# Two row blocks of w_out loaded during the mix, and the first two token tiles multiplied block by block in four banks

## The chip, the core and the metric

The kernel runs on one core of one Trainium2 chip, in one launch. The metric is the device time of the whole program in microseconds. The kernel before takes 2972.97 us, the median of three runs (2965.73 to 2975.23).

## The reference, cut to what matters

The program computes two transformer-like blocks for 1024 tokens of width 1024, in float32. The change lies in the first block, between its two branches and its mixture of experts:

```python
mixed = (jax.nn.sigmoid(g_rwkv) * (o_rwkv @ w_branch_rwkv[l])
         + jax.nn.sigmoid(g_diff) * (o_diff @ w_branch_diff[l]))     # "the mix"
x = x + mixed @ w_out[l]                                             # "mix_out": 1024 x 1024 weights
x = x + hierarchical_moe(rms_norm(x, norm_ffn[l]), ...)              # router, then 32 experts, top 2
```

## The kernel before, in words

Each float32 operand of a large product is split into a rounded part, `hi`, and a rest, `lo` (`split`, lines 188 to 191: ScalarE writes `hi`, then VectorE writes `lo`). A product is then three TensorE matmuls, hi by hi (line 276), the one operand's hi by the other's lo (277), and lo by hi (278).

**The mix** (`mix`, line 812) goes over eight feature blocks `f` and two branches `b`. For each pair it loads 128 columns of a branch weight, splits them, and makes two half products of 12 matmuls each (token halves of 512) into two PSUM buffers with the tag `mm`. VectorE takes each out of PSUM and multiplies it by the gate (837, 839). The result is split straight into `mT[j]`, one tile of 8 KB a partition for each of the eight token tiles `j` (842, 843).

**mix_out** (line 852) loads the eight row blocks `k` of `w_out` (128 x 1024 each, 512 KB), one by one, into two raw buffers `wr`, and splits each into a hi and a lo tile `mx_w`. Then, for each token tile `j`, it forms two products of 512 columns, each of 8 x 3 matmuls, adds them to a tile `xr` of `x` (872), and hands it to the callback: store as `x1`, RMS norm, store as `mo_hn`, transpose, router logits, top 2 (`tile_in`, from line 934). This is the routing of a tile; it is interleaved on all engines with the products of the next tiles.

**The ring.** `mT` are eight of the ten buffers of a pool called the ring (`ring_tile`, line 885). Later users take the buffers in turn: the weights of the experts, loaded by `half` (line 1032) in pieces of 1 MB. Before the change the next two buffers, the ninth and tenth, hold the two halves of the first expert's `w_gate`.

**What sets the order.** The program is recorded in the order of the code. A scheduler with a timeline model then fixes the order of the instructions on each engine; an engine executes its own list in order, and each DMA is issued by SyncE (SP) in the order of its list. A DMA that waits therefore holds back all that stand behind it. Memory of a closed pool is used again by the next one; an instruction that writes there waits for the last reader or writer of that stretch.

Of the kernel before, what the change touches and what calls it, by code (L numbers as in the profile page):

```python
# [11 lines left out]
F32 = mybir.dt.float32  # L12
F32R = mybir.dt.float32r
# [9 lines left out]
T = 1024  # L23
D = 1024
KT = 8
# [783 lines left out]
    es.close()  # L809


def mix(K, o_ds, gate_d, mT):

    nc, tc, ap = K.nc, K.tc, K.ap
    with K.pool(name="mx_i", bufs=1) as ip, K.pool(name="mx_g", bufs=1) as gp, K.pool(name="mx_o", bufs=1) as op:
        oT = [[p.tile([128, 4, T], F32R, name=f"mx_oT{b}{i}") for i in range(2)] for b, p in enumerate((ip, op))]

        def load(b):  # L820
            for k in range(4):
                raw = ip.tile([128, T], F32, name=K.name("mx_raw"), tag="raw", bufs=3)
                nc.sync.dma_start(raw, o_ds[b].rearrange("(k p) t -> k p t", p=128)[k])
                K.split(oT[b][0][:, k], oT[b][1][:, k], raw)

        gts = {}

        def branch(b, f):
            if b == 0:
                gts[f] = gp.tile([128, 2, T], F32, name=K.name("gt"), tag="gt", bufs=3)  # L830
            gt = gts[f]
            w = K.load_w(ip, ap[("w_branch_rwkv", "w_branch_diff")[b]][0], [(f * 128, 128)], kt=4, raw_bufs=3, bufs=4)
            nc.sync.dma_start(gt[:, b], gate_d[b * 1024 + f * 128:b * 1024 + (f + 1) * 128, :])
            for hf in range(2):
                hs = slice(hf * 512, (hf + 1) * 512)
                p = K.gemm_fm(w, 0, 128, oT[b], hf * 512, kt=4)
                nc.vector.scalar_tensor_tensor(gt[:, b, hs], gt[:, b, hs], 1.0, p, op0=OP.add, op1=OP.mult)
                if b:
                    nc.vector.tensor_add(gt[:, 0, hs], gt[:, 0, hs], gt[:, 1, hs])
                    for j in range(hf * 4, hf * 4 + 4):  # L840
                        g, m = gt[:, 0, j * 128:(j + 1) * 128], mT[j]
                        nc.scalar.activation(m[:, 0, f], g, AF.Copy, scale=0.5)
                        nc.vector.scalar_tensor_tensor(m[:, 1, f], g, 0.5, m[:, 0, f].bitcast(F32), op0=OP.mult, op1=OP.subtract)

        load(0)
        branch(0, 0)
        load(1)
        for f in range(8):
            if f < 7:
                branch(0, f + 1)  # L850
            branch(1, f)


def mix_out(K, mT, x, cb):

    nc, tc, ap = K.nc, K.tc, K.ap
    with K.pool(name="mx_w", bufs=1, side="right") as wp:
        his, los = [], []
        for k in range(KT):
            raw = wp.tile([128, D], F32, name=K.name("wr"), tag="wr", bufs=2)  # L860
            nc.sync.dma_start(raw, ap["w_out"][0, k * 128:(k + 1) * 128, :])
            hi, lo = [wp.tile([128, 1, D], F32R, name=f"mx_w{i}{k}") for i in range(2)]
            K.split(hi[:, 0], lo[:, 0], raw)
            his.append(hi)
            los.append(lo)
        w = Parts(his, los, 1)
        for j in range(8):
            xr = wp.tile([128, D], F32, name=K.name("xr"), tag="xr", bufs=3)
            nc.sync.dma_start(xr, x[j * 128:(j + 1) * 128, :])
            for c in range(2):  # L870
                p = K.gemm_tm(w, (mT[j][:, 0], mT[j][:, 1]), 0, 512, c0=c * 512)
                nc.vector.tensor_add(xr[:, c * 512:(c + 1) * 512], xr[:, c * 512:(c + 1) * 512], p)
            cb(j, xr)


# [9 lines left out]
def ring_tile(K, ring, *shape, dt=F32):  # L885

    return ring.tile([128, *shape], dt, name=K.name("we"), tag="w", bufs=RING)
# [1018 lines left out]
def s5_scratch(K, dp):  # L1906
    d = {
        "keep": dp.tile([128, S5Keep.N], F32, name="s5d_keep"),
        "ca": dp.tile([128, 4, 2, 4, 144], F32, name="s5d_ca"),
        "km": dp.tile([32 * 16 * 240], F32, name="s5d_km"),  # L1910
        "wt": dp.tile([128, 4, 2, 4, 128], F32, name="s5d_wt"),
        "ro": dp.tile([128, 4, 2, 4, 128], F32, name="s5d_ro"),
    }
    with K.pool(name="s5z", bufs=1) as zp:
        zero = zp.tile([128, 960], F32, name="s5_zero")
        K.nc.vector.memset(zero, 0.0)
        K.nc.sync.dma_start(dap(d["km"], 0, [[960, 128], [1, 960]]), zero)
    return d
# [261 lines left out]
def branches(K, x, xs_d, gate_d, or_d, od_d):  # L2180

    tc = K.tc
    with K.pool(name="hT", bufs=1) as hp, K.pool(name="bd", bufs=1, space=DRAM) as dd:
        tab_d, qk_d, pd = (dd.tile(list(s), F32, name=f"d_{n}") for n, s in
                            (("tab", (2, 8, 128, 128)), ("qk", (T, 1024)), ("pd", (T, 1536))))
        hT = [hp.tile([128, KT, T], F32R, name=f"hT{i}") for i in range(2)]
        with K.pool(name="wp", bufs=1) as wp, K.pool(name="rp", bufs=1) as rp:
            first_w = lambda i, p: K.load_w_steps(wp, K.ap["w_in"][0], [(RWKV_ORDER[i] * 128, 128)], part=KT, raw_pool=p, raw_bufs=2)
            after, ws = norm_in(K, x, "norm_mix", hT, first_w)
            rwkv_proj(K, hT, wp, xs_d, rp, ws)  # L2190
            with K.issue_after(*after):
                rope_tables(K, tab_d)
                zeros = rwkv_scratch(K, dd)
            rwkv_core(K, xs_d, or_d, zeros)
            rope = norm_rope(K, rp, pd, tab_d, qk_d)
            proj_diff(K, hT, wp, rp, pd, lambda c: rope if c > 1 else iter(()))
            gates = proj_gate(K, hT, wp, rp, gate_d)
            for _ in range(5):
                next(gates)
            diff_attn(K, qk_d, pd[:, 1024:1536], od_d, gates)  # L2200
            for _ in gates:
                pass
# [53 lines left out]
def program(tc, nc, cst, out, **ap):  # L2256
    K = Kern(tc, ap, cst)
    K.setup()
    dd = K.es.enter_context(K.pool(name="dd", bufs=1, space=DRAM))
    dt = lambda n, *s: dd.tile(list(s), F32, name=f"d_{n}")  # L2260
    xs_d, gate_d = dt("xs", 1792, T), dt("gate", 2048, T)
    or_d, od_d, x1_d, y_d, x3_d = dt("or", 512, T), dt("od", 512, T), dt("x1", T, D), dt("y", 2 * T, D), dt("x3", T, D)
    mixT_d, part_d = dt("mixT", 1536, T), dt("part", T, D)
    branches(K, ap["x"][0], xs_d, gate_d, or_d, od_d)
    d5 = s5_scratch(K, dd)
    rings = ExitStack()
    ring = rings.enter_context(K.pool(name="mo_w", bufs=1, side="right"))
    mT = [ring_tile(K, ring, 2, KT, 128, dt=F32R) for _ in range(8)]
    mix(K, [or_d, od_d], gate_d, mT)

    def x1_tiles(cb):
        def put(j, x1):
            nc.sync.dma_start(x1_d[j * 128:(j + 1) * 128, :], x1)
            cb(j, x1)
        mix_out(K, mT, ap["x"][0], put)

    pps = ExitStack()
    pp = Ple(K, pps, ring, dt("pp", T // 2, D))

    def beside():  # L2280
        yield from s5_prep(K, d5)
        yield from pp.late()

    moe(K, ring, x1_tiles, y_d, pp.early(), beside(), pp.weights)
    es = ExitStack()
    hp = es.enter_context(K.pool(name="hU", bufs=1))
    hT = [hp.tile([128, KT, T], F32R, name=f"hU{i}") for i in range(2)]
    ple(K, pp, x1_d, y_d, x3_d, hT)
    pps.close()
    rings.close()  # L2290
    mixers(K, es, hT, d5, mixT_d, part_d, x3_d, out)
    K.close()
# [14 lines left out]
```

## Time and profile before

| what | us |
|---|---|
| median of three runs | 2972.97 |
| their range | 2965.73 to 2975.23 |
| the profiled execution | 2955.07 |
| its span, first to last instruction | 2953.3 |
| TensorE busy in it | 2786.6 (94%) |
| mean granted TensorE clock | 0.970 of full speed |

The profile is of one execution, 17.9 us shorter than the median of the runs. Times in its rows count from the start of the span. PE is TensorE's matmul, PEld its weight load, DVE is VectorE, ACT ScalarE, SP SyncE's DMA queue. In the stage of interest, the mix ends at about 1042 us, mix_out lasts to about 1168 us, and the experts follow.

### The profile page before, as it was taken

What the parts mean: (1) busy time and instruction counts of PE and PEld (TensorE: products, weight loads), DVE (VectorE), ACT (ScalarE), POOL (GpSimd) and SP (SyncE); (2) the same over time, 40 slices, a digit from 0 to 9 for tenths busy, and PEclk for the clock granted to TensorE, in tenths of its full rate; (3) what the DMA queues carried; (4) which work ended last, traced back from release to release, by engine and by line L of the source; (5) the groups of instructions that cost most, each with busy time, mean ns of one, the idle gap of its engine ahead of it and who ended that gap; (6) DMA issues with size and microseconds to landing.
All of it is one profiled execution on the core that took longest, in us unless ns stands there. A gap on an engine that the chain in (4) does not pass through costs nothing. (4 is left out here: it accounts for less than half of the span.)

```text
span 2953.3 us, 47258 instructions
## 1 busy us (share of the span) xinstructions
PE 2786.6 (94%) x18410; PEld 2290.6 (78%) x18410; DVE 1962.3 (66%) x3826; ACT 1314.0 (44%) x2167; POOL 229.2 (8%) x193
## 2 busy tenths in 40 slices
PE   6999999988998989979999999999999999999998
PEld 5888888765776868668777776678888899987776
DVE  4436787654455655769988888569745666768653
ACT  4223332223454221658877877334432335543431
POOL 0000111000000000112122110000000000000000
PEclk9999999987998999989999999999999999999999
DMA  5333343323213465879999996542234444357333
GB/s 182 103 96 90 108 129 115 106 64 99 65 61 139 159 196 186 281 261 376 378 339 336 351 361 241 185 126 88 88 111 129 132 133 146 99 164 225 109 125 132
DMA packets 378146, 503.31 MB, mean 170 GB/s; under 512 B 86039, under 2 KB 234422, under 8 KB 377918
## 3 DMA queue, kind: packets, MB, share of 16 engines
q1 hardware_dynamic: 347742, 458.63, 47.1%
q0 software_dynamic: 11296, 24.57, 2.3%
q10 hardware_dynamic: 18880, 17.05, 1.7%
q8 instruction: 146, 2.39, 0.3%
q14 instruction: 82, 0.67, 0.1%
HBM read 410.26 MB, written 106.68 MB: 175 GB/s over the span
## 5 line engine op out<-in xcount | busy, mean ns | idle before, releaser
L191 DVE TENSOR_TENSOR wh<-we,wh 128x1024 fp32r<-128x1024 f32 x384 | 451.2, 1219 | 62.5 <-ACT wh L190 60.9
L190 ACT ACTIVATE wh<-we 128x1024 fp32r<-128x1024 f32 x384 | 385.7, 1057 | 47.3 <-PE b L278 29.7
L276 PE MATMUL mm<-wh,hU 128*128 128x256 f32 (+1 forms) x768 | 221.7, 291 | 6.8 <-DVE z L1385 4.0
L277 PE MATMUL mm<-wl,hU 128*128 128x256 f32 (+1 forms) x768 | 220.3, 287 | 2.5 <-DVE wl L191 2.5
L278 PE MATMUL mm<-wh,hU 128*128 128x256 f32 (+1 forms) x768 | 218.6, 285 | 0.0
L278 PE MATMUL mm<-wh,hT 128*128 128x256 f32 (+1 forms) x640 | 211.6, 331 | 0.0
L276 PE MATMUL mm<-wh,hT 128*128 128x256 f32 (+1 forms) x640 | 203.0, 334 | 2.3 <-ACT ye L1082 2.3
L276 PE MATMUL mm<-hT,wh 128*128 128x512 f32 x480 | 194.4, 406 | 4.1 <-DVE xs L321 3.9
L277 PE MATMUL mm<-hT,wh 128*128 128x512 f32 x480 | 190.9, 398 | 0.0
L278 PE MATMUL mm<-hT,wl 128*128 128x512 f32 x480 | 189.1, 394 | 0.0
L190 ACT ACTIVATE wh<-wr 128x1024 fp32r<-128x1024 f32 (+2 forms) x102 | 100.9, 992 | 196.9 <-PE mm L277 152.9
L191 DVE TENSOR_TENSOR wl<-wr,wh 128x1024 fp32r<-128x1024 f32 (+2 forms) x102 | 115.9, 1137 | 91.5 <-ACT wh L190 84.4
L276 PEld LDWEIGHTS mm<-wh,hU 128*128 128x128 f32 x768 | 146.0, 191 | 11.0 <-DVE z L1385 5.0
L277 PEld LDWEIGHTS mm<-wl,hU 128*128 128x128 f32 x768 | 146.8, 191 | 5.7 <-DVE wl L191 3.3
L278 PEld LDWEIGHTS mm<-wh,hU 128*128 128x128 f32 x768 | 146.8, 191 | 1.4 <-issue 1.4
L276 PEld LDWEIGHTS mm<-wh,hT 128*128 128x128 f32 x640 | 121.0, 190 | 17.4 <-issue 3.4
L278 PEld LDWEIGHTS mm<-wh,hT 128*128 128x128 f32 x640 | 121.6, 190 | 16.1 <-issue 4.9
L276 PE MATMUL mm<-hU,wh 128*128 128x512 f32 x320 | 129.0, 403 | 4.5 <-ACT wh L190 4.5
L277 PE MATMUL mm<-hU,wh 128*128 128x512 f32 x320 | 127.5, 398 | 0.0
L278 PE MATMUL mm<-hU,wl 128*128 128x512 f32 x320 | 126.6, 396 | 0.0
L276 PEld LDWEIGHTS mm<-hT,wh 128*128 128x128 f32 x480 | 91.3, 191 | 30.2 <-DVE xs L321 4.4
L277 PE MATMUL mm<-wl,hT 128*128 128x256 f32 x384 | 111.1, 290 | 0.0
(704 smaller groups left out, 7062.7 us busy)
## 6 DMA issues: line engine op xcount, KB each, us to landing
we<-w_gate SPq DMA_DIRECT2D x64, 1024.0 KB
we<-w_up SPq DMA_DIRECT2D x64, 1024.0 KB
we<-w_down SPq DMA_DIRECT2D x64, 1024.0 KB
wr<-w_in SPq DMA_DIRECT2D x86, 512.0 KB
d_gate<-gz SPq DMA_DIRECT2D x32, 256.0 KB
gt<-d_gate SPq DMA_DIRECT2D x16, 512.0 KB
x<-d_x SPq DMA_DIRECT2D x16, 512.0 KB
dec<-sd_cum SPq DMA_DIRECT2D x16, 512.0 KB
```

The lines of the kernel that those rows point to most:

```text
L190: self.nc.scalar.activation(hi, src, AF.Copy)
L191: self.nc.vector.tensor_sub(lo, src, hi.bitcast(F32))
L276: nc.tensor.matmul(out, a[0], b[0], start=first, stop=False)
L277: nc.tensor.matmul(out, a[0], b[1], start=False, stop=False)
L278: self.last = nc.tensor.matmul(out, a[1], b[0], start=False, stop=last)
```

## The change

Two of the eight row blocks of `w_out` are loaded and split during the mix: a call `ahead`, after `f == 3` in the code, takes two of the mix's own raw buffers and writes hi and lo into the last two ring buffers. mix_out then loads only the row blocks 2 to 7, with four raw buffers instead of two. The first two token tiles are multiplied together: for each row block, both tiles and both column halves, in four PSUM banks (two with the tag `mm`, two with the tag `b`). Tiles 2 to 7 go as before.

```diff
-def mix(K, o_ds, gate_d, mT):
+def mix(K, o_ds, gate_d, mT, ahead):
...
+            if f == 3:
+                ahead(rawt)
+
+def w_out_rows(K, k, raw, hi, lo):
+    K.nc.sync.dma_start(raw, K.ap["w_out"][0, k * 128:(k + 1) * 128, :])
+    K.split(hi[:, 0], lo[:, 0], raw)
...
-def mix_out(K, mT, x, cb):
+def mix_out(K, mT, x, w2, cb):
...
-        for k in range(KT):
-            raw = wp.tile([128, D], F32, name=K.name("wr"), tag="wr", bufs=2)
+        his, los = [[t[i] for t in w2] for i in range(2)]
+        for k in range(len(w2), KT):
+            raw = wp.tile([128, D], F32, name=K.name("wr"), tag="wr", bufs=4)
...
-        for j in range(8):
...
+        xrs = [load(j) for j in range(2)]
+        ps = [[K.ps(tag=t) for _ in range(2)] for t in ("mm", "b")]
+        for k in range(KT):
+            for j in range(2):
+                for c in range(2):
+                    K.mm3(ps[j][c], (mT[j][:, 0, k], mT[j][:, 1, k]), w.at(k, slice(c * 512, (c + 1) * 512)), k == 0, k == KT - 1)
+        for j in range(2):
             for c in range(2):
+                add(xrs[j], c, ps[j][c])
+            cb(j, xrs[j])
+        for j in range(2, 8):
...
+    wo = [ring_tile(K, ring, 2, 1, D, dt=F32R) for _ in range(2)]
+    wo = [(t[:, 0], t[:, 1]) for t in wo]
+    def ahead(raw):
+        for k in range(2):
+            w_out_rows(K, k, raw(), *wo[k])
```

The scheduler moves more than the code does. In the rows below, `we_9604` and `we_9605` are `mT[0]` and `mT[1]`, `we_9612` and `we_9613` the split row blocks 0 and 1 of `w_out`. On SP, in the middle of the mix, the order before is:

```order
L823 DMA mx_raw_9689<-d_od 128x1024 [waits DMAHW5_49,DVE_49]
L233 DMA wr_9996<-w_branch_diff 128x4x128 [waits DMAHW3_49,DVE_49]
L233 DMA wr_10050<-w_branch_rwkv 128x4x128 [waits DMAHW0_49,DVE_49]
L1032 DMA we_11656<-w_gate 128x4x512 [waits PE_49]
L1032 DMA we_11658<-w_gate 128x4x512 [waits DMAHW6_49,PE_49]
```

and of the change:

```order
L827 DMA mx_raw_9691<-d_od 128x1024 [waits DMAHW5_49,DVE_49]
L862 DMA mx_raw_10051<-w_out 128x1024 [waits DMAHW6_49,DMAHW3_49,DVE_49]
L862 DMA mx_raw_10055<-w_out 128x1024 [waits DMAHW7_49,DVE_49]
L233 DMA wr_9998<-w_branch_diff 128x4x128 [waits DVE_49]
L233 DMA wr_10060<-w_branch_rwkv 128x4x128 [waits DMAHW0_49,DVE_49]
```

The two loads of `w_out` now stand right behind the last input of the mix, and the two of `w_gate` are gone from here; they stand behind all loads of `w_out`. On DVE, the change puts the two lo parts behind the last split of the first feature block, ahead of the next two products that it takes out of PSUM:

```order
L847 SCALAR_TENSOR_TENSOR we_9611<-gt_9643,we_9611 128x128
L191 TENSOR_TENSOR we_9612<-mx_raw_10051,we_9612 128x1024
L191 TENSOR_TENSOR we_9613<-mx_raw_10055,we_9613 128x1024
L841 SCALAR_TENSOR_TENSOR gt_9784<-gt_9784,mm_9806 128x512
L191 TENSOR_TENSOR wl_9964<-wr_9963,wh_9966 128x512
L841 SCALAR_TENSOR_TENSOR gt_9695<-gt_9695,mm_9827 128x512
```

The row L841 of `mm_9806` is the old row L837 that followed at once. On PE, six matmuls of token tile 1 by row block 0 go in behind the product `mm_9827`, and six by row block 1 some 24 matmuls later:

```order
L278 MATMUL mm_9827<-mx_oT_9625,wl_9821 128x512
L276 MATMUL b_10483<-we_9612,we_9605 128x512
L276 MATMUL b_10484<-we_9612,we_9605 128x512
L277 MATMUL b_10483<-we_9612,we_9605 128x512
L278 MATMUL b_10483<-we_9612,we_9605 128x512
L277 MATMUL b_10484<-we_9612,we_9605 128x512
L278 MATMUL b_10484<-we_9612,we_9605 128x512
L276 MATMUL mm_9850<-mx_oT_9625,wh_9823 128x512
```

So 12 matmuls of mix_out now lie inside the mix. On SP, where the mix ends, the order before is:

```order
L861 DMA wr_10431<-w_out 128x1024 [waits DMAHW3_49,DVE_49]
L861 DMA wr_10437<-w_out 128x1024 [waits DMAHW4_49]
L869 DMA xr_10479<-x 128x1024 [waits DMAHW5_49,PE_49]
L869 DMA xr_10623<-x 128x1024 [waits DMAHW6_49]
L869 DMA xr_10767<-x 128x1024 [waits DMAHW7_49]
L861 DMA wr_10443<-w_out 128x1024 [waits DMAHW3_49,DMAHW0_49,DVE_49]
```

and of the change:

```order
L862 DMA wr_10441<-w_out 128x1024 [waits DMAHW3_49,DVE_49,PE_49]
L862 DMA wr_10447<-w_out 128x1024 [waits DMAHW4_49,DVE_49]
L862 DMA wr_10453<-w_out 128x1024 [waits DMAHW5_49]
L862 DMA wr_10459<-w_out 128x1024 [waits DMAHW6_49]
L882 DMA xr_10477<-x 128x1024 [waits DMAHW7_49]
L882 DMA xr_10479<-x 128x1024 [waits DMAHW0_49]
L882 DMA xr_10765<-x 128x1024 [waits DMAHW1_49]
L862 DMA wr_10465<-w_out 128x1024 [waits DMAHW3_49,DMAHW2_49,DVE_49]
```

The wait for PE has moved from the first load of `x` to the first load of `w_out`: the pool is laid out anew, and its first raw buffer now lies where the mix keeps its last lo weights. By its count this wait, like the old one of `xr_10479`, is for the last product of the mix. On PE, behind the mix, the change has:

```order
L278 MATMUL mm_10482<-we_9612,we_9604 128x512
L276 MATMUL mm_10482<-we_9613,we_9604 128x512
L277 MATMUL mm_10482<-we_9613,we_9604 128x512
L278 MATMUL mm_10482<-we_9613,we_9604 128x512
L276 MATMUL mm_10481<-mx_w_10442,we_9604 128x512
L276 MATMUL mm_10482<-mx_w_10442,we_9604 128x512
L276 MATMUL b_10483<-mx_w_10442,we_9605 128x512
L276 MATMUL b_10484<-mx_w_10442,we_9605 128x512
L277 MATMUL mm_10481<-mx_w_10443,we_9604 128x512
L278 MATMUL mm_10481<-mx_w_10442,we_9604 128x512
```

The first four of these rows end the 12 matmuls of token tile 0 by row blocks 0 and 1; with `mx_w_10442` (hi of row block 2) begin the 72 of both tiles by row blocks 2 to 7, 12 for each, four of them before the lo part is needed.

## Rows read from the trace of the kernel before

**Rows 1.** The page: busy us and share of the span, by engine.
```profile
PE 2786.6 (94%) x18410; PEld 2290.6 (78%) x18410; DVE 1962.3 (66%) x3826; ACT 1314.0 (44%) x2167; POOL 229.2 (8%) x193
```

**Rows 2.** Windows: us from:to, length, busy us (instructions) by engine, clock, DMA share, GB/s.
```profile
969.00:1042.00 73.00, 72.24 (x317) 59.16 (x316) 47.76 (x114) 20.01 (x70) 1.92 (x3) 1.00 0.47 146
1042.00:1070.00 28.00, 17.74 (x49) 10.44 (x50) 13.42 (x23) 9.15 (x12) 0.00 (x0) 0.88 0.55 195
1070.00:1168.00 98.00, 98.00 (x530) 83.91 (x529) 50.92 (x237) 18.66 (x46) 3.88 (x7) 1.00 0.55 177
```

**Rows 3.** Timeline of PE: start us, us, engine, line, operation [idle before].
```profile
1034.73 0.39 PE L278 MATMUL mm<-mx_oT,wl 128*128 128x512 f32 x1
...
1041.53 0.39 PE L278 MATMUL mm<-mx_oT,wl 128*128 128x512 f32 x1
1045.31 0.73 PE L276 MATMUL mm<-mx_w,we 128*128 128x512 f32 x2 [3.39 <-ACT mx_w L190]
...
1069.72 0.50 PE L276 MATMUL mm<-mx_w,we 128*128 128x512 f32 x1 [0.32 <-DVE xr L872]
```

**Rows 4.** Waits in 1042 to 1070 us: us in total, times, longest.
```profile
ACT mx_w L190 <- DMA wr<-w_out: 14.2, 5, 5.0
```

**Rows 5.** Timeline of SP: DMAs issued at the end of the mix.
```profile
1038.76 0.85 SPq L861 DMA_DIRECT2D wr<-w_out  x2
1041.72 1.28 SPq L869 DMA_DIRECT2D xr<-x  x3
...
1054.74 0.33 SPq L861 DMA_DIRECT2D wr<-w_out  x1
...
1062.37 0.33 SPq L861 DMA_DIRECT2D wr<-w_out  x1
```

**Rows 6.** Timeline of ACT and PE: the sixth and the eighth row block.
```profile
1060.03 1.06 ACT L190 ACTIVATE mx_w<-wr 128x1024 fp32r<-128x1024 f32 x1 [1.75 <-DMA wr<-w_out]
...
1065.84 1.06 ACT L190 ACTIVATE mx_w<-wr 128x1024 fp32r<-128x1024 f32 x1 [1.69 <-DMA wr<-w_out]
...
1066.95 0.73 PE L276 MATMUL mm<-mx_w,we 128*128 128x512 f32 x2 [0.29 <-ACT mx_w L190]
1068.21 0.50 PE L277 MATMUL mm<-mx_w,we 128*128 128x512 f32 x1 [0.53 <-DVE mx_w L191]
```

**Rows 7.** Windows inside mix_out's first tile, columns as in rows 2.
```profile
1042.00:1047.00 5.00, 1.17 (x4) 0.69 (x5) 4.42 (x15) 2.80 (x6) 0.00 (x0) 1.00 1.02 415
1047.00:1050.00 3.00, 3.00 (x9) 2.36 (x8) 0.65 (x1) 0.00 (x0) 0.00 (x0) 0.52 0.89 268
...
1054.00:1057.00 3.00, 3.00 (x9) 2.32 (x8) 0.71 (x1) 0.00 (x0) 0.00 (x0) 0.50 0.72 220
1057.00:1069.00 12.00, 8.02 (x26) 4.06 (x25) 4.92 (x5) 4.23 (x4) 0.00 (x0) 0.99 0.35 121
```

**Rows 8.** Timeline of DVE and ACT in the mix.
```profile
965.52 1.23 DVE L191 TENSOR_TENSOR mx_oT<-mx_raw,mx_oT 128x1024 fp32r<-128x1024 f32 x1
...
973.28 0.91 ACT L842 ACTIVATE we<-gt 128x128 fp32r<-128x128 f32 x4 [0.29 <-DVE gt L839]
...
974.78 0.69 DVE L843 SCALAR_TENSOR_TENSOR we<-gt,we 128x128 fp32r<-128x128 f32 x3
976.67 0.69 DVE L837 SCALAR_TENSOR_TENSOR gt<-gt,mm 128x512 f32<-128x512 f32 x1 [1.21 <-PE mm L278]
...
979.39 0.69 DVE L837 SCALAR_TENSOR_TENSOR gt<-gt,mm 128x512 f32<-128x512 f32 x1 [1.43 <-PE mm L278]
```

**Rows 9.** Timeline of ACT: the first split of an expert's weights.
```profile
1187.02 3.88 ACT L190 ACTIVATE wh<-we 128x1024 fp32r<-128x1024 f32 x4
```

**Rows 10.** Timeline of SP among the experts: loads of many small pieces.
```profile
1253.56 2.80 SPq L1722 DMA_DIRECT2D s_b<-s_b_re  x1
1256.40 15.22 SPq L1722 DMA_DIRECT2D s_b<-s_b_im  x1
```

**Rows 11.** Waits of PE over the whole span: the longest.
```profile
PE t L1730 <- DMA craw<-s_c_re: 15.1, 2, 14.5
```

More of the change, by code (lines that the diff above doesn't have):

```diff
@@ L818, in mix, with rawt @@
         oT = [[p.tile([128, 4, T], F32R, name=f"mx_oT{b}{i}") for i in range(2)] for b, p in enumerate((ip, op))]
+        def rawt():
+            return ip.tile([128, T], F32, name=K.name("mx_raw"), tag="raw", bufs=3)
         def load(b):
             for k in range(4):
-                raw = ip.tile([128, T], F32, name=K.name("mx_raw"), tag="raw", bufs=3)
+                raw = rawt()
                 nc.sync.dma_start(raw, o_ds[b].rearrange("(k p) t -> k p t", p=128)[k])
@@ L851, in mix @@
             branch(1, f)
-def mix_out(K, mT, x, cb):
+            if f == 3:
[4 more added lines that the diff above has]
+def mix_out(K, mT, x, w2, cb):
     nc, tc, ap = K.nc, K.tc, K.ap
     with K.pool(name="mx_w", bufs=1, side="right") as wp:
-        his, los = [], []
-        for k in range(KT):
-            raw = wp.tile([128, D], F32, name=K.name("wr"), tag="wr", bufs=2)
-            nc.sync.dma_start(raw, ap["w_out"][0, k * 128:(k + 1) * 128, :])
+        his, los = [[t[i] for t in w2] for i in range(2)]
+        for k in range(len(w2), KT):
+            raw = wp.tile([128, D], F32, name=K.name("wr"), tag="wr", bufs=4)
             hi, lo = [wp.tile([128, 1, D], F32R, name=f"mx_w{i}{k}") for i in range(2)]
-            K.split(hi[:, 0], lo[:, 0], raw)
+            w_out_rows(K, k, raw, hi, lo)
             his.append(hi)
@@ L866, in mix_out, with load, add @@
         w = Parts(his, los, 1)
-        for j in range(8):
+        def load(j):
             xr = wp.tile([128, D], F32, name=K.name("xr"), tag="xr", bufs=3)
             nc.sync.dma_start(xr, x[j * 128:(j + 1) * 128, :])
-            for c in range(2):
-                p = K.gemm_tm(w, (mT[j][:, 0], mT[j][:, 1]), 0, 512, c0=c * 512)
-                nc.vector.tensor_add(xr[:, c * 512:(c + 1) * 512], xr[:, c * 512:(c + 1) * 512], p)
+            return xr
+        def add(xr, c, p):
+            nc.vector.tensor_add(xr[:, c * 512:(c + 1) * 512], xr[:, c * 512:(c + 1) * 512], p)
+        xrs = [load(j) for j in range(2)]
[5 more added lines that the diff above has]
+        for j in range(2):
+            for c in range(2):
+                add(xrs[j], c, ps[j][c])
+            cb(j, xrs[j])
+        for j in range(2, 8):
+            xr = load(j)
+            for c in range(2):
+                add(xr, c, K.gemm_tm(w, (mT[j][:, 0], mT[j][:, 1]), 0, 512, c0=c * 512))
             cb(j, xr)
@@ L2268, in program @@
     mT = [ring_tile(K, ring, 2, KT, 128, dt=F32R) for _ in range(8)]
-    mix(K, [or_d, od_d], gate_d, mT)
+    wo = [ring_tile(K, ring, 2, 1, D, dt=F32R) for _ in range(2)]
[3 more added lines that the diff above has]
+            w_out_rows(K, k, raw(), *wo[k])
+    mix(K, [or_d, od_d], gate_d, mT, ahead)
     def x1_tiles(cb):
@@ L2274, in put @@
             cb(j, x1)
-        mix_out(K, mT, ap["x"][0], put)
+        mix_out(K, mT, ap["x"][0], wo, put)
     pps = ExitStack()
```

## The prediction

> **What bounds the kernel now.** I read the page's shares first: PE is busy for 94% of the span [rows 1], so time is to be had only where PE is not busy. The windows by stage show where that is: in the mix PE is busy for 72.24 of 73 us, while the tiles are routed for 98.00 of 98, and between the two lies a stretch of 28 us with 17.74 busy and a mean clock of 0.88 [rows 2]. The timeline of PE gives its ends: the last matmul of the mix starts at 1041.53, the first by `w_out` at 1045.31, and the second token tile begins at 1069.72 [rows 3]. The waits name what ends last there: ACT, which splits the row blocks, waits 14.2 us for the loads of `w_out` [rows 4]. SP shows why they are late: two are issued at 1038.76, and the others wait for a raw buffer, the sixth until 1054.74, the eighth until 1062.37 [rows 5]. The stage is bound by a chain of load and split through two buffers.
>
> **The change part by part.** All times are those of the profiled execution, 2955.07 us (span 2953.3 and 1.8 around it).
>
> *The price of a matmul.* From 1034.73 to 1041.53 lie 30 starts [rows 3], so 0.2267 us each; the 48 of a token tile take 10.88 us, 12 take 2.72.
>
> *Before.* Tile 0 is over and tile 1 begins at 1069.72. Tile 1 alone needs 10.88 us, so both would be done at 1080.60, the routing rows between them left out here and below.
>
> *In the mix.* Twelve matmuls of tile 1 move in. PE has no gap there, so the mix ends 2.72 us later, its last matmul starting at 1044.25 and ending 0.39 us on, at 1044.64. The splits of row blocks 0 and 1 are 2 x 1.06 us of ACT and 2 x 1.23 of DVE (durations as in [rows 6] and [rows 8]). Their loads wait for the splits of the mix's second and third `d_od` input; the later ends at 966.75 [rows 8]. With the longest time that a load takes in these rows, 5.29 us from issue to split for the sixth row block [rows 5, 6], they are there by 972.1, before ACT reaches them at 974.19 [rows 8]. DVE has a hole of 1.21 us up to 976.67, so its two splits, from 975.5 to 977.9, put off the next eviction by 1.3 us; DVE then still makes its next one at 979.39, ahead of which it had waited 1.43 us for PE [rows 8]. There are two PSUM buffers and a half product lasts 2.72 us, so PE is not held: I take nothing. If the delay went through to PE it would cost 1.3. The matmuls themselves stand at about 979.4, behind data of 976.7.
>
> *After the mix.* Nothing is lost at first: 12 matmuls of tile 0 are ready and run to 1047.20 (1044.25 + 0.23 + 2.72). But the first load now waits for the last product of the mix, as the loads of `x` did, which were issued at 1041.72, 0.2 us after that product's start [rows 3, 5]. So it goes at 1044.67, not at 1038.76: it loses the head start that the old first load had. The eighth row block gives the rest: issue at 1062.37, split at 1065.84, hi used at 1066.95, lo at 1068.21 [rows 5, 6], that is 3.47, 4.58 and 5.84 us. So hi of row block 2 is there at 1049.25 and lo at 1050.51. PE stands from 1047.20 to 1049.25 (2.05 us), makes four matmuls by 1050.16, stands 0.35, and makes the other eight by 1052.32. From here it should not wait: the loads of row blocks 3 to 5 are issued 0.43 us apart and take 1.26 us each at 415 GB/s [rows 7], so they land by 1052, ahead of a PE that needs 2.72 us for each. Row blocks 6 and 7 come behind three tiles of `x`: seven transfers from 1046.9 are over at 1055.7, these two at 57.0 and 58.2, split 2.37 us later; PE wants them at 1060.5 and 1063.2. So both tiles end at 1052.32 + 5 x 2.72 = 1065.92, and the stage gains 1080.60 - 1065.92 = 14.7 us. Without any stand it would be 17.1.
>
> *What follows.* PE is full while the tiles are routed, 98.00 us with seven tiles' products, 76.2, and 21.8 of routing [rows 2]. The change does the same routing beside six tiles, in 87.1 us. DVE has 50.9 us to do in it, 58%, so I count no loss; the upper price is one tile's routing that PE has to wait for, 21.8 / 7 = 3.1. The chain from the last tile to the experts is the same.
>
> *The ring and SP.* `w_gate` of expert 0 leaves the mix and is loaded when tiles 0 and 1 are done, about 1066. It is first wanted when ACT splits it, at 1187.02 [rows 9], 1172 after the change: over 100 us for 2 MB, hidden. The last two halves that wait for `mT[7]` and the two `w_out` buffers belong to expert 1, which comes later still.
>
> *Order elsewhere.* The scheduler swaps some tens of instructions among the experts and in the last stage. I take nothing, with 3 us either way, from the size of a stand of this kind (3.39 in [rows 3]).
>
> Sum: 14.7 us less, 2940.4 in the time of the profile. The median is 17.9 us above the profile, and I leave this distance as it is: 2972.97 - 14.7 = 2958.3. With 1.8 for a slow first load (5.29 instead of 3.47), 1.3, 3.1 and 3 on one side, the gain falls to 5.5; with 2.4 and 3 on the other it is 20.
>
> **A rule against the change.** The granted clock fell to half twice in tile 0 of before, 0.52 in 1047 to 1050 and 0.50 in 1054 to 1057, each behind stands of PE, and not in 1057 to 1069, where PE was busy for 8.02 of 12 us in short pieces [rows 7]. The Trainium skill, in TensorE: Matmul & The Clock Gate, section HAM oscillation, says that a loop which waits for a load at each step of the contraction loses its clock at every step, and advises to do all steps of one token tile before waiting for a load. The change does the opposite, with row blocks outside and tiles inside; by that rule it would run the blocks at half clock. By the rows, each load now feeds 12 matmuls, not 6, 2.72 us against 1.26, so PE should wait only for the first. The two cases are rivals below.
>
> **Rivals.**
> 1. *The clock falls once, behind the stand of 2.05 us.* For it: the stands are like those before the second fall. Against: full activity up to the stand. A clock of 0.52 for 3.00 us [rows 7] costs 0.48 x 3.00 = 1.4 us, two such falls 2.9: 2960 to 2961.
> 2. *The clock is down through all row blocks.* At 0.50 [rows 7] the 72 matmuls from row block 2 on take twice their time, 72 x 0.2267 = 16.3 us more. Time 2974.6, no change. Against it is that only one wait is left.
> 3. *The gain is handed back among the experts.* PE's longest wait anywhere is 14.5 us, for small loads [rows 11] that stand on SP behind a load whose issue takes 15.22 us, while its twin takes 2.80 [rows 10]. [...] If the twin is held as well, 12.4 us are lost: 2970.7. Against it: loads and compute there move together.
> 4. *Slower: the products in the mix.* PE, ACT and DVE take their lists in order, and all the mix stands behind the two new splits. ACT has cover until 974.2 and DVE's holes of 1.21 and 1.43 us [rows 8] give some 2 us more. A load that lands later than 976.2 stops the mix one for one; from 990.9 on the change is slower than before, and from 24 us after issue on that is. At 1000, 2982. No load of this size in the rows takes more than 5.29 us.
> 5. *No stand at all,* since the first load's wait falls earlier than I read it: gain 17 to 20, 2954.
>
> **How the numbers follow.** Chances: forecast 0.56, clock falls once or twice 0.18, clock down throughout 0.05, handed back 0.12, slower 0.04, no stand 0.05. The likeliest gives 2958; its own range is 2953 to 2967. Runs of one kernel lie up to 7 us from their median here. The range of 2949 to 2970 takes in the first rival, the last, and the spread, and leaves out most of the others, 0.2. What a measurement of this kernel can tell from no change is 0.3%, 8.9 us. The forecast passes it with 0.88 (6 us of room), the first rival with 0.8, the last with 1, handed back with 0.1: 0.49 + 0.14 + 0.05 + 0.01, 0.7. Slower is 0.05, from the slower rival and a little of the spread, no change 0.25.
>
> **What would show it.** Right: the last matmul of the mix starts near 1044.3; the first load of `w_out` on SP behind the mix near 1044.7; a stand of PE of some 2 us, then 72 matmuls at 0.227 us; the third tile from about 1066; the first split of expert weights near 1172; the span near 2939. Wrong: a gap of PE near 976 to 986; a clock of 0.5 behind 1047; PE waiting for routing between 1066 and 1153; a longer wait for the small loads among the experts. The forecast falls if the stage gains its 14.7 us and the span does not.

## The result and the profile after

The changed kernel takes 2958.15 us (median of 11 runs, 2950.12 to 2968.72), the kernel before 2971.71 (11 runs, 2964.85 to 2975.80): 13.6 us less, a ratio of 0.9949 with a 95% interval of 0.9937 to 0.9962. Forecast were 2958.3 and a gain of 14.7.

The profiled execution alone would say the opposite: its span is 2958.8 us, that of before 2953.3. So the first thing to read is where the two profiles part. The first matmul of the mix, in the timeline of PE, stands ahead of everything that the change touches. Before:

```profile
948.49 0.80 PE L276 MATMUL mm<-mx_oT,wh 128*128 128x512 f32 x1 [3.06 <-ACT wh L190]
```

After:

```profile
966.61 0.80 PE L276 MATMUL mm<-mx_oT,wh 128*128 128x512 f32 x1 [3.06 <-ACT wh L190]
```

The first split of expert weights, in the timeline of ACT of after (that of before is in [rows 9]):

```profile
1192.03 2.94 ACT L190 ACTIVATE wh<-we 128x1024 fp32r<-128x1024 f32 x3
```

The mix begins 18.1 us later in the profile of after, behind the same instructions. From there to the experts it is 225.4 us, where before had 1187.02 - 948.49 = 238.5: the stretch that holds the change is 13.1 us shorter. What follows to the end of the span is alike in these two, 1766.3 before and 1766.8 after. I call the middle number, from the first product of the mix to the first expert split, **the stretch**. In repeats of one kernel it stays within 0.7 us (before, two profiles) and 2.1 us (the change, three), while the spans of the same profiles lie 21.0 and 7.8 us apart.

More than half of the 18.1 us are lost in one region. A row of 31 matmuls of line 606 starts at 640.33 before and at 647.24 after, 6.9 us later; the first product behind the attention that follows starts at 725.18 and 742.66, 17.5 us later. The windows of 640 to 760 us (columns as in [rows 2]) show the region. Before:

```profile
640.00:760.00 120.00, 99.31 (x753) 69.65 (x754) 54.62 (x151) 40.58 (x108) 5.29 (x4) 0.77 0.25 81
```

After:

```profile
640.00:760.00 120.00, 98.10 (x741) 70.50 (x739) 51.59 (x145) 33.59 (x88) 4.28 (x3) 0.66 0.24 75
```

The granted clock, the number ahead of the DMA share, is 0.77 and 0.66. Between its two levels, 1.2 and 2.4 GHz, that is 55 us of the 120 at the lower one before and 82 after. Over the whole way to the mix it is 86 and 119 us. If work at the lower level takes twice as long, these 33 us more cost 17 of the 18.1, an estimate; what brings the clock down there is not shown. It is no doing of the change, as the repeats below show.

In the stage itself the steps up to row block 2 stand where the prediction put them, 18.1 us later, to 0.2 us; the third token tile comes 1.9 us later than that. Timeline of PE after, which answers to [rows 3]:

```profile
1062.38 0.40 PE L278 MATMUL mm<-mx_oT,wl 128*128 128x512 f32 x1
...
1065.13 0.39 PE L278 MATMUL mm<-we,we 128*128 128x512 f32 x1
1067.50 0.73 PE L276 MATMUL mm<-mx_w,we 128*128 128x512 f32 x2 [1.98 <-ACT mx_w L190]
...
1068.76 0.50 PE L277 MATMUL mm<-mx_w,we 128*128 128x512 f32 x1
...
1085.91 0.39 PE L276 MATMUL mm<-we,we 128*128 128x512 f32 x1
```

The mix's last product starts at 1062.38, the ready products end at 1065.5, PE stands 1.98 us, row block 2 begins at 1067.50 (its lo at 1068.76), and the third token tile at 1085.91. That is 23.5 us from the mix's last product to the third tile, where before needed 40.1 (1041.53 to 1081.66). Its third tile, in the timeline of PE before:

```profile
1081.66 0.39 PE L276 MATMUL mm<-mx_w,we 128*128 128x512 f32 x1
```

The timeline of SP after, answering to [rows 5]:

```profile
1062.80 1.75 SPq L862 DMA_DIRECT2D wr<-w_out  x4
...
1068.73 1.76 SPq L862 DMA_DIRECT2D wr<-w_out  x2
```

And that of ACT, at the split of row block 2:

```profile
1066.39 1.06 ACT L190 ACTIVATE mx_w<-wr 128x1024 fp32r<-128x1024 f32 x1 [1.22 <-DMA wr<-w_out]
```

The first load goes 0.42 us behind the start of the mix's last product and its split begins 3.59 us after the issue. The windows of after (answering to [rows 2] and [rows 7]):

```profile
987.00:1063.00 76.00, 75.31 (x330) 61.97 (x331) 50.06 (x116) 21.89 (x72) 1.92 (x3) 1.00 0.37 114
1063.00:1086.00 23.00, 20.96 (x85) 16.49 (x84) 11.17 (x22) 7.27 (x10) 0.00 (x0) 0.93 0.53 206
1086.00:1174.00 88.00, 88.00 (x492) 76.00 (x490) 50.70 (x241) 18.51 (x47) 3.87 (x7) 1.00 0.64 216
1069.00:1073.00 4.00, 4.00 (x12) 3.09 (x12) 2.48 (x3) 2.11 (x2) 0.00 (x0) 0.57 1.02 416
1073.00:1086.00 13.00, 13.00 (x59) 10.76 (x58) 4.80 (x6) 2.13 (x2) 0.00 (x0) 1.00 0.23 93
```

The stage of 28 us with 17.74 busy has become one of 23 with 20.96; PE is busy for 75.31 of 76 us in the mix and for 88.00 of 88 while six tiles are routed. One thing is not as forecast: behind the stand the clock is 0.57 for 4 us, and PE does 12 matmuls there instead of 17 or 18.

### The profile page after: what moved, and what is told of

It reads as the page before. It is cut to its first block, busy times and chain, and to the rows that moved or that the text cites. A ratio compares the mean times of both kernels' runs of the same rounds, so it can differ in the third digit from the quotient of the medians.

```text
span 2958.8 us, 47258 instructions
## 1 busy us (share of the span) xinstructions
PE 2797.2 (95%) x18410; PEld 2306.6 (78%) x18410; DVE 1961.4 (66%) x3826; ACT 1314.0 (44%) x2167; POOL 229.5 (8%) x193
## 5 line engine op out<-in xcount | busy, mean ns | idle before, releaser
L276 PEld LDWEIGHTS mm<-wh,hT 128*128 128x128 f32 x640 | 122.4, 192 | 17.9 <-issue 3.4
```

The source lines that it names most:

```text
L276: nc.tensor.matmul(out, a[0], b[0], start=first, stop=False)
```

## The experiments

Eleven runs. All have the same 7797 matmuls ahead of the mix, so each is also a sample of that part. Each altered kernel but one (e6, again in e10) was profiled once, so a difference of the stretch below some 2 us between two of them may be chance. The stretch is read in each as above, from the two rows of the timelines; medians stand beside the kernel before timed on the same chip.

| run | mix begins | stretch | median | before | ratio (95%) |
|---|---|---|---|---|---|
| before | 948.5 | 238.5 | 2971.71 | | |
| e8, before again | 967.4 | 239.2 | one run, 2976.07 | | |
| after | 966.6 | 225.4 | 2958.15 | 2971.71 | 0.9949 (0.9937 to 0.9962) |
| e7, change again | 966.7 | 225.7 | one run, 2967.57 | | |
| e11, change timed | 960.8 | 223.7 | 2958.96 | 2971.67 | 0.9952 (0.9934 to 0.9970) |
| e1, buffers alone | 958.7 | 232.9 | 2965.44 | 2976.86 | 0.9977 (0.9964 to 0.9990) |
| e2, early + buffers | 957.4 | 232.5 | 2968.79 | 2976.86 | 0.9989 (0.9975 to 1.0004) |
| e3, order + buffers | 969.0 | 228.9 | 2963.30 | 2976.86 | 0.9959 (0.9946 to 0.9972) |
| e4, order + early | 957.4 | 227.8 | 2961.11 | 2976.86 | 0.9962 (0.9947 to 0.9977) |
| e9, one buffer | 962.7 | 239.7 | one run, 2970.61 | | |
| e5, six buffers | 965.4 | 222.4 | 2962.56 | 2974.51 | 0.9953 (0.9935 to 0.9971) |
| e6, late rows early | 966.1 | 221.3 | 2956.39 | 2974.51 | 0.9943 (0.9921 to 0.9965) |
| e10, the same again | 967.8 | 221.8 | 2956.84 | 2971.67 | 0.9940 (0.9919 to 0.9962) |

By the time itself every timed kernel but e2 is faster than before (the interval of e2 reaches past 1). Against the changed kernel's first timing only e1 (barely) and e2 have intervals that lie wholly above; e3, e4, e5, e6 and e10 can't be told from it by time, and what is said of them below goes by the stretch.

**The kernels again, unaltered.** No edit. For e7, e8 and e11 was expected:

> The changed kernel once more, unaltered. My theory: what comes before the mix is the same work in both kernels and differs between executions by the clock alone; the mix begins anywhere from 945 to 970 us, and the stretch from its first product to the first expert split is 225.4 again, within 1.5 us (without the fall of the clock 223.9). Rival (the change slows the work before the mix): the mix begins at 966 again.

> The kernel before once more, unaltered. My theory: the mix begins anywhere from 945 to 970 us, and the stretch from its first product to the first expert split is 238.5 within 1.5 us. Rival (the profile of before was of its own kind from the start on): the mix begins near 948 again, and the stretch differs by more.

> The changed kernel, unaltered, beside the former on one chip. My theory: 225.5 us within 1 from the first product of the mix to the first expert split; median 13 us below before, 4 above the former.

The second profile of before begins its mix at 967.4, at a clock of 0.65 in 640 to 760; its span is 2974.3. Its timeline of PE:

```profile
967.43 0.80 PE L276 MATMUL mm<-mx_oT,wh 128*128 128x512 f32 x1 [3.14 <-ACT wh L190]
```

Its timeline of ACT at the first expert split:

```profile
1206.67 1.05 ACT L190 ACTIVATE wh<-we 128x1024 fp32r<-128x1024 f32 x1
```

And its window:

```profile
640.00:760.00 120.00, 97.79 (x738) 70.27 (x735) 51.13 (x145) 33.00 (x87) 4.28 (x3) 0.65 0.24 76
```

So the late start is no effect of the change: the same code starts its mix at 948.5 or 967.4, and the profile of before that the prediction rests on was the earliest of 13. The rival of e7 had named 966 and got it (966.7), but the change began its mix at 960.8 in e11, and before at 967.4 in e8: the rival fell. The stretch of before is the same within 0.7 us.

The third profile of the change shows what the clock costs. The timeline of PE in e11, from the mix's last product over row block 2 to the third tile:

```profile
1056.17 0.40 PE L278 MATMUL mm<-mx_oT,wl 128*128 128x512 f32 x1
...
1061.30 0.50 PE L276 MATMUL mm<-mx_w,we 128*128 128x512 f32 x1 [1.99 <-ACT mx_w L190]
...
1078.12 0.39 PE L276 MATMUL mm<-we,we 128*128 128x512 f32 x1
```

And its window behind the stand:

```profile
1062.00:1066.00 4.00, 3.93 (x18) 2.92 (x17) 2.36 (x3) 2.14 (x3) 0.00 (x0) 1.00 1.03 417
```

The stand is the same, 1.99 us, and the clock stays at 1.00: 18 matmuls in the 4 us where after did 12. From the mix's last product to the third tile it takes 21.95 us, in after 23.53, in e7 23.35 (there too the clock fell, 0.66 in 1068 to 1073). The fall costs 1.4 to 1.6 us and comes in two of three executions. The stretch without it was 223.7; for e11 225.5 within 1 had been expected, so this missed by 0.8.

**Which of the three edits makes the gain.** The change is three: two row blocks early, four raw buffers, and the order by blocks. With four raw buffers and all eight split row blocks, mix_out's pool would take 92 KB a partition (four raw buffers and three tiles of `x` of 4 KB, eight pairs of hi and lo of 8), against 84 before; the kernels with four keep the two ring buffers for blocks 0 and 1.

Buffers alone (e1): the call of `ahead` goes, all blocks are loaded behind the mix, and the tiles are multiplied one by one.

```diff
-            if f == 3:
-                ahead(rawt)
...
-        for k in range(len(w2), KT):
+        for k in range(KT):
             raw = wp.tile([128, D], F32, name=K.name("wr"), tag="wr", bufs=4)
+            if k < len(w2):
+                w_out_rows(K, k, raw, *w2[k])
+                continue
...
-        xrs = [load(j) for j in range(2)]
-        ps = [[K.ps(tag=t) for _ in range(2)] for t in ("mm", "b")]
-        for k in range(KT):
...
-        for j in range(2, 8):
+        for j in range(8):
```

> Only the four raw buffers of the change: all eight row blocks are loaded behind the mix, and both token tiles are multiplied one after the other. From the first product of the mix to the first split of expert weights the profile of before has 238.5 us, that of the changed kernel 225.4. My theory (three edits, none of which makes the gain alone): the loads come about 1.3 us apart until the fourth, the others wait for splits and for x; tile 0 ends some 20 us behind the mix instead of 28, so this stretch is 230 to 232, the time 6 to 8 us below before. Rival (the raw buffers make the gain): 225 to 227, 12 to 13 us below. Rival (early loading makes it): 237 to 239, no gain.

Early and buffers (e2) has only the last part of this diff, from `xrs` on; order and buffers (e3) has only the part ahead of it. Order and early with two buffers (e4) changes one number:

```diff
-            raw = wp.tile([128, D], F32, name=K.name("wr"), tag="wr", bufs=4)
+            raw = wp.tile([128, D], F32, name=K.name("wr"), tag="wr", bufs=2)
```

> Two row blocks loaded and split during the mix, four raw buffers, but tile 0 and then tile 1, as before: each later load feeds 6 matmuls (1.36 us), not 12. My theory: tile 0 waits for every block and ends about 19 us behind the mix, tile 1 takes its 10.9 us after it: 229 to 231 us from the first product of the mix to the first expert split, 8 to 9 us below before. Rival (the early blocks make the whole gain): 225 to 226, 13 below. Rival (they only save the first load, about 4 us): 234.

> Both tiles block by block in four banks, four raw buffers, but all eight row blocks loaded behind the mix. My theory: PE stands some 5 us for the first load, then does 96 matmuls in 21.8 us, plus 1.5 to 3 us of lowered clock behind the stand: 228 to 231 us from the first product of the mix to the first expert split, 8 to 10 below before. Rival (the order makes the whole gain): 225 to 226. Rival (the clock stays at half through the blocks, since PE waits for each): 240 or more, no gain.

> The changed kernel with two raw buffers in place of four, the number before: each pair of row blocks waits for the splits of the pair ahead of it. In before a block came every 3.8 us at this; PE needs 2.72 for the two tiles. My theory: the loads behind the first pair come just as PE wants them, it waits about 0.5 us once or twice: 225.5 to 228 us from the first product of the mix to the first expert split, the time at most 2 above the changed kernel. Rival (four buffers are needed): 231 or more. Rival (the clock falls wherever PE waits for a load): 235 to 240, the granted clock 0.5 through the blocks.

By the stretch, the buffers alone save 5.6 us (e1). The order on top of them saves 4.0 (e3) and early loading on top of both 3.5 (after), 5.6 + 4.0 + 3.5 = 13.1 in all. Early loading on top of the buffers without the order saves 0.5 (e2), less than repeats differ by. Part of the 3.5 is the clock, which is 0.57 from 1065 to 1073 us in e3, a fall twice as long as in after; against e11, which has none, the saving is 5.2. No single edit makes the gain, as expected. e1 missed its range by 0.9 us, and e2 missed by more: it was to save 8 to 9 us against before and saved 6.1. The waits of PE show why. In e1 there is one long one, for the first load behind the mix:

```profile
1057.35 1.22 PE L276 MATMUL mm<-we,we 128*128 128x512 f32 x2 [5.06 <-ACT we L190]
```

In e2 there are two, for row block 2 and for row block 6:

```profile
1055.71 0.88 PE L276 MATMUL mm<-mx_w,we 128*128 128x512 f32 x2 [2.19 <-ACT mx_w L190]
...
1065.77 0.74 PE L276 MATMUL mm<-mx_w,we 128*128 128x512 f32 x2 [2.35 <-ACT mx_w L190]
```

And the windows behind them:

```profile
1056.00:1060.00 4.00, 3.62 (x10) 2.48 (x10) 3.90 (x4) 2.99 (x3) 0.00 (x0) 0.57 1.02 418
1066.00:1073.00 7.00, 6.48 (x15) 4.38 (x15) 3.58 (x4) 1.56 (x2) 0.00 (x0) 0.53 0.12 5
```

With 6 matmuls per block, 1.36 us, PE catches up with the loads twice, behind row blocks 1 and 5 (blocks 6 and 7 are issued behind three tiles of `x`), and both times the clock falls. Without the order, early blocks only split the wait of e1 in two. The order by blocks gives each load 2.72 us of work; on top of it one stand is left (1.98 in after, 4.61 in e3), and the early blocks pay.

In e4 the stretch is 2.4 us longer than after, 1.6 of them inside the mix (97.4 us from its first product to its last, in after 95.8, and in e9, with still fewer buffers, 95.9; so the buffers did not make it). The timeline of PE shows most of it, a wait for an input of the mix, ahead of anything that the number of buffers touches:

```profile
975.91 0.73 PE L276 MATMUL mm<-mx_oT,wh 128*128 128x512 f32 x2 [1.27 <-ACT mx_oT L190]
```

The same wait is 0.29 us in after and 0.88 in e8, the unaltered kernel before: the mix's own length differs from one execution to the next. The stands of e4 behind the mix:

```profile
1059.77 0.72 PE L276 MATMUL mm<-mx_w,we 128*128 128x512 f32 x2 [1.85 <-ACT mx_w L190]
1067.40 0.73 PE L276 MATMUL mm<-mx_w,we 128*128 128x512 f32 x2 [1.57 <-ACT mx_w L190]
```

And the window from the first of them to the third tile:

```profile
1057.00:1079.00 22.00, 18.39 (x77) 13.50 (x76) 9.67 (x18) 6.92 (x9) 0.00 (x0) 1.00 0.56 207
```

A second stand of 1.57 us appears, for the pair that waits for the first pair's splits (waits of about 0.5 were expected), and the clock is 1.00 all through. From the mix's last product to the third tile e4 takes 24.4 us, 2.5 more than e11, where the clock did not fall either.

**One buffer (e9).**

```diff
-            raw = wp.tile([128, D], F32, name=K.name("wr"), tag="wr", bufs=4)
+            raw = wp.tile([128, D], F32, name=K.name("wr"), tag="wr", bufs=1)
```

> The changed kernel with one raw buffer: each of the six later row blocks is loaded only when the one ahead of it has been split, 3.6 us from issue to split, 1.06 for hi and 1.23 for lo, so one comes every 6 us, while PE has 2.72 us of work per block. My theory (the gain hangs on loads that come faster than 2.72 us): from the mix's last product to the third tile 38 to 41 us, as in before, from the first product of the mix to the first expert split 240 to 243 us: nothing left of the gain. Rival (the order alone carries it): below 230. On the clock: if it falls wherever PE waits for a load at each step, it is 0.5 through all six blocks, and a block's 12 products take 5.4 us; if it falls only in some of the stands, they take 2.7 to 4.

The stretch is 239.7, 0.3 under the range and no shorter than in before (238.5 and 239.2): with loads that come every 5.8 us the order by blocks and the early blocks are worth nothing. The starts of row blocks 2 to 7 in the timeline of PE:

```profile
1062.33 0.73 PE L276 MATMUL mm<-mx_w,we 128*128 128x512 f32 x2 [0.65 <-ACT mx_w L190]
1069.32 1.22 PE L276 MATMUL mm<-mx_w,we 128*128 128x512 f32 x2 [3.62 <-ACT mx_w L190]
1075.19 0.74 PE L276 MATMUL mm<-mx_w,we 128*128 128x512 f32 x2 [0.38 <-ACT mx_w L190]
1081.03 0.84 PE L276 MATMUL mm<-mx_w,we 128*128 128x512 f32 x2 [2.48 <-ACT mx_w L190]
1086.77 0.72 PE L276 MATMUL mm<-mx_w,we 128*128 128x512 f32 x2 [1.12 <-ACT mx_w L190]
1092.62 0.73 PE L276 MATMUL mm<-mx_w,we 128*128 128x512 f32 x2 [2.50 <-ACT mx_w L190]
```

And four windows:

```profile
1068.00:1075.00 7.00, 5.49 (x12) 3.80 (x12) 1.22 (x1) 1.97 (x2) 0.00 (x0) 0.52 0.24 75
1075.00:1082.00 7.00, 4.27 (x15) 2.92 (x16) 2.21 (x2) 1.20 (x2) 0.00 (x0) 0.97 0.26 75
1082.00:1085.00 3.00, 3.00 (x8) 2.24 (x8) 0.24 (x1) 0.00 (x0) 0.00 (x0) 0.51 0.50 167
1085.00:1096.00 11.00, 7.26 (x28) 4.73 (x27) 3.80 (x5) 2.15 (x3) 0.00 (x0) 1.00 0.17 50
```

PE waits ahead of every block. The clock falls at the waits of 3.62 and 2.48 us, but not at that of 2.50: from 1085 on it is 1.00. Where it falls, the slower products only shorten the next wait (0.38 and 1.12), so the time per block is the load's either way.

**Taking the stand away.** Six raw buffers (e5) are again the one number:

```diff
-            raw = wp.tile([128, D], F32, name=K.name("wr"), tag="wr", bufs=4)
+            raw = wp.tile([128, D], F32, name=K.name("wr"), tag="wr", bufs=6)
```

The pool's first raw buffer then lies 8 KB lower, away from the mix's last weights, and its load need not wait for the mix's last product.

> The changed kernel with six raw buffers: the first of them then lies 8 KB lower, on tiles that the mix gave up long before, so the first two loads behind the mix need not wait for its last product, and the two row blocks that came behind x come ahead of it. My theory: the stand of 2.14 us is the load of row block 2 (3.6 us from issue to split); with it gone, PE waits only for the split itself, which ACT begins after its last copies of the mix: a stand of about 1.0 us. From the first product of the mix to the first expert split 222.7 to 224.4 us instead of 225.4, the lower value if the clock does not fall behind the shorter stand. Rival (the stand is set by the copies and splits on ACT and DVE): 225.4, no change. The median can show this only as 0 to 3 us less.

The mix's last product and the first one by row block 2 in the timeline of PE, the loads of `w_out` in that of SP, and their first splits in that of ACT:

```profile
1061.14 0.40 PE L278 MATMUL mm<-mx_oT,wl 128*128 128x512 f32 x1
1064.93 0.74 PE L276 MATMUL mm<-mx_w,we 128*128 128x512 f32 x2 [0.65 <-ACT mx_w L190]
1058.28 4.82 SPq L862 DMA_DIRECT2D wr<-w_out  x6
1063.84 2.94 ACT L190 ACTIVATE mx_w<-wr 128x1024 fp32r<-128x1024 f32 x3
```

The first load goes 2.86 us ahead of the mix's last product instead of 0.42 behind it, and ACT splits it without a wait, right behind its last copies of the mix. The stand shrinks from 1.98 to 0.65 us, the clock stays at 1.00 (1061 to 1082), and the stretch is 222.4, 0.3 below the range. That is 3.0 below after, and 1.2 below e11, where the clock stayed up too: more than half of the 3.0 can be the clock. In e6 the two row blocks of the mix are, besides, the last two of `w_out`:

```diff
-            w_out_rows(K, k, raw(), *wo[k])
+            w_out_rows(K, KT - 2 + k, raw(), *wo[k])
...
-        for k in range(KT):
+        for n, k in enumerate((6, 7, 0, 1, 2, 3, 4, 5)):
```

> As the kernel with six raw buffers, but the two row blocks that are loaded in the mix are the last two of w_out, not the first two: their products need the last features of the mix, so 18 of the 24 matmuls stand behind the mix's last product and not 12. My theory: they cover 4.1 us, in which row block 2 is split: no stand, no lowered clock; from the first product of the mix to the first expert split 221 to 222.5 us, about 4 below the changed kernel. Rival (the products need copies by ACT and DVE that end 1 to 3 us behind the mix, and PE waits for these instead): 224 to 226. Rival (the clock falls anyway): 223.

> The kernel with six raw buffers and the last two row blocks loaded in the mix, once more, timed beside the changed kernel on one chip. My theory: 221.3 us again from the first product of the mix to the first expert split, within 1, and the median 4 us below the changed kernel, if 4 us can be told at all. Rival (it is handed back later): the medians are equal.

Timeline of PE in e6, from the mix's last product over the first one by a block loaded behind the mix to the third tile:

```profile
1060.14 0.40 PE L278 MATMUL mm<-mx_oT,wl 128*128 128x512 f32 x1
...
1064.47 0.62 PE L276 MATMUL mm<-mx_w,we 128*128 128x512 f32 x2
...
1080.83 0.39 PE L276 MATMUL mm<-mx_w,we 128*128 128x512 f32 x1
```

And the windows:

```profile
1060.00:1066.00 6.00, 6.00 (x28) 4.93 (x27) 4.85 (x15) 3.98 (x8) 0.00 (x0) 1.00 0.89 322
1066.00:1081.00 15.00, 15.00 (x68) 12.41 (x67) 7.00 (x8) 3.46 (x4) 0.00 (x0) 1.00 0.38 139
```

No stand, no fall: 20.7 us to the third tile, which are 90 matmuls at 0.23. The stretch is 221.3, in e10 221.8, some 4 us below after and 2 below e11. The medians are 2956.39 and 2956.84, in e10 2.1 us below the changed kernel timed beside it, where 4 were expected. The intervals overlap, so that this kernel is faster than the changed one is shown in the stretch only.

## Why the prediction was right, and where it was not

**The mix: right.** Its products span 93.04 us before and 95.77 after, 2.73 more; 2.72 were forecast for the 12 matmuls, and no stall through ACT and DVE. That the two agree to 0.01 is luck: the same span is 94.1 in e8, 95.95 in e7 and 95.4 in e11.

**The stand: right.** The wait of the first load that came in with the pool's layout is there: issue 0.42 us behind the start of the last product, hi needed 5.12 behind it (forecast 5.00), a stand of 1.98 by the row, or 2.14 from where the next product could have started, as the forecast's 2.05 was counted. The forecast's issue is 0.42 behind too, but the text derives only 0.2 of it, from the loads of `x` before; the other 0.23, one matmul, has no reason in it, and that it fits is luck. That it is this wait is shown by e5, which removes it and two thirds of the stand.

**"72 matmuls at 0.2267": wrong in two profiles of three.** The step that failed is the choice between the forecast and the first rival, by "full activity up to the stand". The clock fell behind this stand in after and in e7, not in e11. In e11 the stretch is 14.9 us below the first profile of before, where the forecast has 14.7; in after it is 13.1, in e7 12.8 (all three are 0.7 more against e8). The price, 1.4 to 1.6, is about the 1.4 that the first rival had been given. A rival that holds in two executions of three was worth more than the 0.18 it got beside the forecast's 0.56.

**The rule against the change.** The clock was not down through the row blocks: at most 4 us of them in after. The Trainium skill, in TensorE: Matmul & The Clock Gate, section HAM oscillation, has it that a loop whose matmuls in each step of the contraction take less time than the wait for the next load loses its clock at every step, and that all steps of one token tile should go first. The changed kernel is not that case: it waits at one block of six. No run here shows a fall at every step: e9, with 2.72 us of work and waits of 0.38 to 3.62 at all six blocks, loses the clock at two, and e4 waits twice and keeps it. Blocks outside were the better order (e3 against e1: 4.0 us), since each load then has twice the work behind it.

**What follows: right.** PE has no gap while the tiles are routed, and from the third tile to the experts it is 105.4 us before and 106.1 after (106.4 and 106.3 in e7 and e11). The load of `w_gate` goes at 1085.20, the first split at 1192.03. The third rival, the small loads among the experts, is read from SP's timeline after (answering to [rows 10]):

```profile
1257.88 5.72 SPq L1752 DMA_DIRECT2D s_b<-s_b_re  x1
1263.65 12.95 SPq L1752 DMA_DIRECT2D s_b<-s_b_im  x1
```

And from the waits of PE (answering to [rows 11]; us in total, times, longest):

```profile
PE t L1760 <- DMA craw<-s_c_re: 13.9, 2, 13.0
```

Both issues together take 18.7 us, before 18.0 (17.9 to 19.8 in the 13 profiles: where one is longer, the other is shorter), and the longest wait is 13.0, before 14.5 (13.3 in e7, 14.5 in e11): these loads hand nothing back. The rest of the program is less steady than one pair of profiles suggests: behind the stretch it takes 1766.3 and 1767.6 us in the two profiles of before, but 1766.8, 1773.3 and 1773.6 in after, e7 and e11. The longer two have a lower clock in 2640 to 2780 us, 0.91 and 0.93 (0.99 in after, 1.00 and 0.96 in before and e8). Whether the change has a part in this is not shown: the other altered kernels take anything from 1763.7 (e3) to 1778.1 us (e5), and e6 and e10, which load two blocks early as well, 1768.6 and 1767.3.

**The span: wrong.** "Near 2939" was a promise about one execution. 2940.4 had been worked out for the profile's time and 2960.57 was measured: 18.1 of the 20.2 us between them are the later start of the mix, 1.6 the stretch, where the clock fell, and 0.5 the rest of the program. Leaving the 17.9 us between profile and median as they were was right for the median and says what the profile was: an execution with a lucky first 950 us.

**The median.** 13.6 us in the first timing, 12.7 in e11, against 14.7: near what the stretch gives with the clock falling in some executions. These differences lie within the intervals. That 2958.15 stands 0.15 us from the forecast's 2958.3 is luck: before came out 1.3 us lower in eleven runs (2971.71) than in the three that the forecast started from, and the gain 1.1 smaller.

## What to carry to other kernels

When the weights of a stage arrive one load at a time, count the work that each load releases against the time that a load takes: early loads helped here only after the order gave each block two tiles' work (0.5 us of the stretch without it, 3.5 with it, in one profile each). After any change of buffer counts, look whose memory the first buffer now lies on, since the wait for its last reader can become the stage's first stall. Compare two profiles by the stretch between two instructions on either side of the change, not by their spans.

## Not expected of the hardware

- The same instructions reach the mix anywhere from 948.5 to 969.0 us in 13 profiles. The two of before, 948.5 and 967.4, have 86 and 119.5 us at the lower clock on the way there, and part of the difference lies in one region (0.77 and 0.65 in 640 to 760 us).
- A stand of 1.98 to 2.00 us of PE behind the same full mix was followed by a lower clock in two executions and not in a third; nor were the stands of 1.85 and 1.57 us in e4. The length of a stand alone does not tell whether the clock falls.
